# A shared SBUF port in the clocks of a program planner, and tiles split when they exist

## The chip, the cores and the metric

The kernel runs on one NeuronCore of a Trainium2 chip. Its engines each work through a queue of their own: TensorE (PE, with its weight loads shown apart as PEld), VectorE (DVE), ScalarE (ACT), GpSimd (POOL) and SyncE (SP), which here issues the DMA transfers. The metric is the device time of one execution in microseconds, less is better.

## What is computed

Two blocks of a network, one after the other, on 1,024 tokens of width 1,024, all in fp32. The first is a gated DeltaNet layer (8 query/key heads, 16 value heads of 128), the second holds 4 differential attention heads and 4 mLSTM heads whose outputs are merged. Cut to what matters for the time:

```python
def gated_deltanet(h, w_in, conv_w, a_log, dt_bias, norm_w, w_out):
    proj = h @ w_in
    qkv, z, b_lin, a_lin = jnp.split(proj, [...], axis=-1)
    qkv = jax.nn.silu(causal_depthwise_conv(qkv, conv_w))
    ...
    t_mat = lax.linalg.triangular_solve(l_mat, eye, left_side=True, lower=True, unit_diagonal=True)
    u = t_mat @ (v * beta);  w = t_mat @ (kb * jnp.exp(gc))
    ...
    def step(state, inp):                       # scan over chunks
        v_new = uc - wc @ state
        o = qd @ state + qkc @ v_new
        state = state * gl + kd.T @ v_new
    o = rms_norm(o, norm_w) * jax.nn.silu(z)
    return o @ w_out

x = x + gate * gated_deltanet(rms_norm(x) * (1 + scale) + shift, ...)    # shift, scale, gate from c @ ada_w
x = rms_norm(x, final_g)
proj = rms_norm(x, norm_pre) @ w_in_2           # 2nd block
ya = rms_norm(diff_attention(qa, ka, va)) * silu(za)
yb = rms_norm(sigmoid(ob) * mlstm(conv(qb), conv(kb), vb, ig, fg)) * silu(zb)
out = (sigmoid(ga) * (ya @ w_a) + sigmoid(gb) * (yb @ w_b)) @ w_out_2
return x + rms_norm(out, norm_post)
```

## The kernel before

**Products.** A large product (a projection of 128 columns, the output product) is cut into steps of three matmuls of 128x512: both operands are split into a high and a low half of fewer bits, and high times high, low times high and high times low are added in PSUM (`proj`, `yps`). A weight slab arrives by DMA (`wraw`); ACT rounds it to the high half (`whi`), and `split_lo` gives the subtraction for the low half (`wlo`) to POOL or to DVE, whichever the clocks below call free. The activations are split the same way (`hid_hi`, `hid_lo`; `ohl`; `h2hl`, whose source is `hv`).

**The first block** goes through eight head pairs, 0 to 7. Each pair has a chain: the convolution of q, k and v on DVE, six taps (`scalar_tensor_tensor` on `qT`, `kT`, `vT`, out of the PSUM tile of the projection), transposes on PE (`g`), decay tiles `E` from `gb`, matrices `U`, then the triangular solve (`levels`: `pG`, `pVT`, `pV`, small matmuls in bursts, and between them the rows `vtmp`, `Vl` on DVE, copied as `Ul` and passed through DRAM to `VTinv`), then the scan over chunks (`pst`, `po`, `pks`, `ptx`), and `finish` (norm, times z). The chain of the next pair's solve runs beside the scan of the one before. After pair 7 the output product is finished (`yps`).

**The second block** normalises the token halves r = 0 and 1 (`norm_tokens`: `x1`, `h2`, eight tiles `hv` each), projects them, and runs the gates of the mLSTM (`fgt`, `sp_z`, `sp_q`), the mLSTM chunks and the attention. From about 1,300 us on its products fill PE to the end.

**What sets the order.** Every instruction is recorded through `Engine.run`, so one line, L183, stands for all of them in the profile, and instructions are told apart by their tiles. The order on each engine is that of recording. `Pace` keeps an estimated clock for each engine while the program is recorded: `issue` starts an instruction at the later of its engine's clock and the time its operands are ready, and moves the clock on by `cost`. When the chain wants an instruction whose start is later than TensorE's clock, `Engine.run` calls `net.fill()`, which puts one step of background work (a product from the queue) ahead of it, and again, until TensorE's estimated clock has caught up or there is nothing to put. A product can be unable to go on: only two PSUM tiles hold products, and some of them wait in the plan for a pair's scan. Other work (weight splits, PSUM evacuations, the rows of the solve) waits in four lists and is recorded by `defer()` when the estimated clocks say that it would start without delay. A step's whole count of instructions is the same however these are mixed; the clocks decide the order, and which engine does a subtraction.

## Time and profile before

| | us |
|---|---|
| median of the runs (3) | 2027.89 |
| least and most of them | 2026.89, 2030.8 |
| the profiled execution | 2023.4 |
| its span | 2021.7 |
| PE busy in the span | 1942.5 |
| DVE, ACT, POOL busy | 1108.1, 909.0, 522.7 |

The profiled execution took 1.7 us more than its span, and 4.5 us less than the median. Two things besides work make up PE's time: the stretches in which it has nothing to run, and those in which it runs at a lower granted clock, in which it counts as busy.

### The profile page before, as it was taken

The numbers are of one execution on the slowest core, as the hardware profiler recorded it, in microseconds if no ns is written. First come the engines' busy times: TensorE is split into PE (matmuls) and PEld (weight loads), VectorE is DVE, ScalarE is ACT, GpSimd is POOL, SyncE is SP. The second block draws the span as 40 slices with busy tenths as digits, with TensorE's granted clock in tenths as the row PEclk, the third lists the DMA queues.
The fourth block names the chain that finished last, engine by engine and source line by source line (L and its number), as shares of the span: only waits on it lengthen the run. The fifth ranks groups of instructions, "written<-read, shape, count | busy, mean of one in ns | idle before, by whom it ended". The sixth has DMA issues, their size and how long they took to land. (4 is left out here: it accounts for less than half of the span.)

```text
span 2021.7 us, 29926 instructions
## 1 busy us (share of the span) xinstructions
PE 1942.5 (96%) x11105; PEld 1595.0 (79%) x11105; DVE 1108.1 (55%) x2639; ACT 909.0 (45%) x2103; POOL 522.7 (26%) x439
## 2 busy tenths in 40 slices
PE   6999999999999999999999799999999999999998
PEld 3778877877778787877778578888888888888887
DVE  3585877877858585843474665666434434000224
ACT  5444464544444544554355355565444444111222
POOL 2211111111111111123555221111334335323320
PEclk8999999999999999989999899999999999999999
DMA  8123313233313231324453311111111111211133
GB/s 281 46 53 67 80 46 82 59 72 89 78 43 72 48 72 35 69 106 144 170 207 106 93 43 32 32 27 32 48 53 48 53 37 47 52 47 48 51 116 125
DMA packets 262977, 152.13 MB, mean 75 GB/s; under 512 B 106314, under 2 KB 238123, under 8 KB 262831
## 3 DMA queue, kind: packets, MB, share of 16 engines
q1 hardware_dynamic: 262830, 150.22, 26.6%
q8 instruction: 88, 1.44, 0.3%
q14 instruction: 59, 0.48, 0.1%
HBM read 125.98 MB, written 24.20 MB: 74 GB/s over the span
## 5 line engine op out<-in xcount | busy, mean ns | idle before, releaser
L183 POOL TENSOR_TENSOR wlo<-wraw,whi 128x512 fp32r<-128x512 f32 x245 | 327.7, 1338 | 1259.1 <-ACT whi L183 1210.3
L183 PE MATMUL proj<-h2hl,whi 128*128 128x512 f32 (+1 forms) x1696 | 537.2, 400 | 7.5 <-ACT first L183 5.2
L183 ACT CAST whi<-wraw 128x512 fp32r<-128x512 f32 x292 | 178.6, 614 | 419.4 <-PE proj L183 212.7
L183 PEld LDWEIGHTS proj<-h2hl,whi 128*128 128x128 f32 (+1 forms) x1696 | 307.3, 189 | 66.7 <-ACT first L183 6.0
L183 PE MATMUL proj<-hid_hi,whi 128*128 128x512 f32 x768 | 336.6, 438 | 4.4 <-DVE vT L183 3.2
L183 PE MATMUL proj<-h2hl,wlo 128*128 128x512 f32 x832 | 326.2, 392 | 0.6 <-POOL wlo L183 0.6
L183 PE MATMUL proj<-hid_hi,wlo 128*128 128x512 f32 x768 | 304.4, 396 | 1.9 <-DVE wlo L183 1.9
L183 PE MATMUL proj<-hid_lo,whi 128*128 128x512 f32 x768 | 303.0, 395 | 0.0
L183 PEld LDWEIGHTS proj<-h2hl,wlo 128*128 128x128 f32 x832 | 156.6, 188 | 35.1 <-POOL wlo L183 1.1
L183 PE MATMUL yps<-whi,ohl 128*128 128x512 f32 x512 | 175.1, 411 | 6.7 <-ACT ohl L183 3.1
L183 PEld LDWEIGHTS proj<-hid_hi,wlo 128*128 128x128 f32 x768 | 145.8, 190 | 35.3 <-DVE wlo L183 2.5
L183 PEld LDWEIGHTS proj<-hid_hi,whi 128*128 128x128 f32 x768 | 146.4, 191 | 30.0 <-issue 5.4
L183 PEld LDWEIGHTS proj<-hid_lo,whi 128*128 128x128 f32 x768 | 147.1, 192 | 21.2
L183 PEld LDWEIGHTS yps<-whi,ohl 128*128 128x128 f32 x512 | 98.8, 194 | 30.4 <-DVE yT L183 3.3
L183 PE MATMUL yps<-wlo,ohl 128*128 128x512 f32 x256 | 102.8, 402 | 3.3 <-POOL wlo L183 2.5
L183 ACT ACT_TABLE_LOAD x75 | 96.2, 1283 | 20.1 <-DVE vT L183 8.7
L183 DVE TENSOR_TENSOR wlo<-wraw,whi 128x512 fp32r<-128x512 f32 x45 | 48.5, 1082 | 86.8 <-ACT whi L183 86.5
L183 ACT ACTIVATE qs<-pks,egc 128x128 f32<-128x128 f32 x112 | 35.0, 363 | 133.4 <-DVE xv L183 101.6
L183 DVE TENSOR_TENSOR vtmp<-Vl,Ul 128x126 f32<-128x126 f32 (+22 forms) x248 | 77.8, 314 | 9.5 <-DMA Ul<-ud 4.7
L183 DVE TENSOR_TENSOR merged<-proj,gate 128x1024 f32<-128x1024 f32 x8 | 9.8, 1220 | 130.0 <-PE proj L183 130.0
L183 ACT ACTIVATE prob<-prob,mx 128x128 f32<-128x128 f32 (+7 forms) x64 | 49.6, 776 | 59.1 <-DVE mx L183 57.6
L183 DVE TENSOR_TENSOR Vl<-Vl,vtmp 128x126 f32<-128x126 f32 (+22 forms) x248 | 71.1, 287 | 9.1
(372 smaller groups left out, 3382.0 us busy)
## 6 DMA issues: line engine op xcount, KB each, us to landing
wraw<-in_w_in SPq DMA_DIRECT2D x112, 256.0 KB, 2.8
wraw<-in_gdn_w_in SPq DMA_DIRECT2D x96, 256.0 KB, 2.8
wraw<-in_gdn_w_out SPq DMA_DIRECT2D x64, 256.0 KB, 3.2
adaw<-in_ada_w SPq DMA_DIRECT2D x16, 512.0 KB, 8.6
odram<-z SPq DMA_DIRECT2D x16, 512.0 KB, 3.0
oraw<-odram SPq DMA_DIRECT2D x30, 256.0 KB, 3.0
xin<-in_x SPq DMA_DIRECT2D x8, 512.0 KB, 4.6
Ul<-ud SPq DMA_DIRECT2D x16, 256.0 KB, 3.4
```

Source lines behind the costliest of these rows:

```text
L183: return f(*args, **kw)
```

## The change

`Pace` gets a record of the last twelve intervals in which VectorE and GpSimd, each, held the port to SBUF that they share (`port`). An instruction of GpSimd counts as using it unless it is a memset, one of VectorE if more than one of its inputs lies in SBUF and is larger than 128 elements in all (`shared`). Such an instruction's estimated start is moved behind every interval of the other engine that it falls into (`port_free`). The estimated cost of the scan operation is doubled. In the output product's last round, `split_h2` no longer splits the tile of h with a fixed number for each head, but the first tile that exists and is not yet split, and what is left is split after the round or where the tile is made. No instruction's arithmetic changes, and no instruction is added or taken away: on PE, 9,305 rows before and after.

```diff
--- before.py
+++ after.py
@@ -43,6 +43,7 @@
         self.dma = 0.0
         self.slots, self.seen, self.count = {}, {}, {}
         self.table = self.group = None
+        self.port = dict(vector=deque(maxlen=12), gpsimd=deque(maxlen=12))
 
     def box(self, ap):
 
@@ -96,6 +97,19 @@
             else:
                 tile_.append([p0, p1, f0, f1, 0.0, t, eng])
 
+    def shared(self, eng, op, ins):
+
+        if eng == "gpsimd":
+            return op != "memset"
+        return eng == "vector" and sum("PSUM" not in str(a.space) and a.ap[0][1] * a.ap[-1][1] > 128 for a in ins) > 1
+
+    def port_free(self, eng, start):
+
+        for a, b in sorted(self.port["gpsimd" if eng == "vector" else "vector"]):
+            if a <= start < b:
+                start = b
+        return start
+
     def cost(self, eng, op, outs, ins, args):
         n = 1
         for _, c in outs[0].ap[1:]:
@@ -113,6 +127,8 @@
                 return 0.03
             return max(0.42 * k, 0.84e-3 * m) if ins[0].dtype == F32R else max(1.68 * k, 1.68e-3 * m)
         if eng == "vector":
+            if op == "tensor_tensor_scan":
+                k *= 2
             return 0.07 + 1.04 * k + (0.06 if op == "scalar_tensor_tensor" else 0)
         if eng == "scalar":
             f = args.get("func", None)
@@ -150,7 +166,12 @@
             end = self.dma + 1.0
         else:
             f = dict(func=args[2]) if op == "activation" else {}
+            shared = self.shared(eng, op, ins)
+            if shared:
+                start = self.port_free(eng, start)
             end = self.t[eng] = start + self.cost(eng, op, outs, ins, f)
+            if shared:
+                self.port[eng].append((start, end))
         src = "dma" if op == "dma_start" else eng
         self.note(src, bo, end, True)
         self.note(src, bi, end, False)
@@ -1432,8 +1453,9 @@
             self.osplit(1, h + 2)
 
         def split_h2(h):
-            if 1 <= h <= KD:
-                self.h2split(h - 1, 0)
+            if h:
+                for k in self.unsplit_h()[:1]:
+                    self.h2split(k, 0)
 
         def gen_a():
             while not all(j.ready for j in self.held):
@@ -1456,9 +1478,15 @@
             yield from rounds(1, 0, every, split1)
             psum(1, 1)
             yield from rounds(1, 1, every, split_h2)
+            self.past.add("out")
+            for k in self.unsplit_h():
+                self.h2split(k, 0)
 
         self.out_a, self.out_b, self.out_c = Job(), Job(), Job()
         self.out_a.gen, self.out_b.gen, self.out_c.gen = gen_a(), gen_b(), gen_c()
+
+    def unsplit_h(self):
+        return [k for k in range(KD) if (k, 0) in self.hv and self.h2[k][0] is None]
 
     def h2split(self, k, r):
         v = self.hv[k, r]
@@ -1542,8 +1570,8 @@
             v = sp.tile([128, 512], F32, name="hv", tag="hv", bufs=8)
             nc.vector.tensor_scalar(v, p, self.p("norm_pre", k), None, op0=OP.mult)
             self.hv[k, r] = v
-            if r:
-                self.h2split(k, 1)
+            if r or "out" in self.past:
+                self.h2split(k, r)
             yield 1
```

What moves is told by the order of the two programs at three places. In all rows the line is `Engine.run`, L183 before and L204 now.

The first place is VectorE around 105 us, before the first pair's solve: the six taps of the convolution of v (`vT`), the matrices `U`, and the decay tiles `E` of the next pair. Before:

```order
L183 TENSOR_TENSOR b2d<-b_940,dl 128x8
L183 SCALAR_TENSOR_TENSOR U<-kk,b_940,E 128x128 x16
L183 SCALAR_TENSOR_TENSOR vT<-proj,convw,vT 128x511
L183 SCALAR_TENSOR_TENSOR E<-gb,gc,past_778 128x128 x4
L183 SCALAR_TENSOR_TENSOR vT<-proj,convw,vT 128x512
L183 SCALAR_TENSOR_TENSOR E<-gb,gc,past_778 128x128 x4
L183 SCALAR_TENSOR_TENSOR vT<-proj,convw,vT 128x510
L183 SCALAR_TENSOR_TENSOR vT<-proj,convw,vT 128x512
L183 SCALAR_TENSOR_TENSOR vT<-proj,convw,vT 128x509
L183 SCALAR_TENSOR_TENSOR vT<-proj,convw,vT 128x512
```

and now:

```order
L204 SCALAR_TENSOR_TENSOR vT<-proj,convw,vT 128x512
L204 COPY ktok<-g 128x512
L204 SCALAR_TENSOR_TENSOR vT<-proj,convw,vT 128x510
L204 TENSOR_SCALAR rk_956<-ssk 128x8
L204 RECIPROCAL rk_956<-rk_956 128x8
L204 TENSOR_TENSOR b_954<-beta,rk_956 128x8
L204 TENSOR_TENSOR b2d<-b_954,dl 128x8
L204 TENSOR_TENSOR b_954<-beta,rk_956 128x8
L204 TENSOR_TENSOR b2d<-b_954,dl 128x8
L204 SCALAR_TENSOR_TENSOR U<-kk,b_954,E 128x128 x16
L204 SCALAR_TENSOR_TENSOR vT<-proj,convw,vT 128x512
L204 SCALAR_TENSOR_TENSOR E<-gb,gc,past_781 128x128 x4
```

Three taps of six (two of them in these rows, the first stands just ahead) have moved ahead of the small operations on `rk` and `b` and of the sixteen on `U`.

The second place is TensorE at the end of the first pair's scan, between the last projection matmuls that can run there and the next pair's solve (`pG`); `g` are transposes, `v` what the scan gave, `vT` the next pair's values. Before, from the transposes of `v` on:

```order
L183 MATMUL g<-ident,v 128x128 x8
L183 MATMUL proj<-hid_hi,whi 128x512
L183 MATMUL proj<-hid_lo,whi 128x512
L183 MATMUL proj<-hid_hi,wlo 128x512
L183 MATMUL proj<-hid_hi,whi 128x512
L183 MATMUL proj<-hid_lo,whi 128x512
L183 MATMUL proj<-hid_hi,wlo 128x512
L183 MATMUL g<-ident,vT 128x128 x8
```

and now, the whole of it from the last projection matmul to `pG`:

```order
L204 MATMUL proj<-hid_hi,wlo 128x512
L204 MATMUL g<-ident,v 128x128 x16
L204 MATMUL g<-ident,vT 128x128 x4
L204 MATMUL gb<-grow,gsel 128x512
L204 MATMUL g<-ident,vT 128x128 x4
L204 MATMUL gb<-grow,gsel 128x512 x2
L204 MATMUL g<-ident,vT 128x128 x4
L204 MATMUL gb<-grow,gsel 128x512
L204 MATMUL g<-ident,vT 128x128 x4
L204 MATMUL pG<-VTinv,U 32x32 x32
```

From the last `po` of the scan to `pG` the program before has 48 projection matmuls, between the transposes for the most part, and now 18, all of them ahead of the transposes; the others stand earlier, most of them in the first pair's stage (108 in one run ahead of the first `pG` instead of 87, and 3 inside it).

The third place is TensorE at the start of the solve of pair 3; pair 6 reads much the same (at pair 4 some steps stood there already, with the `gb`). Before:

```order
L183 MATMUL pG<-VTinv,U 32x32 x32
L183 MATMUL gb<-grow,gsel 128x512
L183 MATMUL pVT<-G,Vinv 32x32
L183 MATMUL proj<-hid_hi,whi 128x512
L183 MATMUL proj<-hid_lo,whi 128x512
L183 MATMUL proj<-hid_hi,wlo 128x512
L183 MATMUL pV<-Vinv,G 32x32 x2
```

and now:

```order
L204 MATMUL pG<-VTinv,U 32x32 x32
L204 MATMUL proj<-hid_hi,whi 128x512
L204 MATMUL proj<-hid_lo,whi 128x512
L204 MATMUL proj<-hid_hi,wlo 128x512
L204 MATMUL proj<-hid_hi,whi 128x512
L204 MATMUL proj<-hid_lo,whi 128x512
L204 MATMUL proj<-hid_hi,wlo 128x512
L204 MATMUL pVT<-G,Vinv 32x32
L204 MATMUL proj<-hid_hi,whi 128x512
```

Two background steps stand between `pG` and the first `pVT` in the place of one `gb`, whose four stand ahead of the solve now.

## Rows read from the trace of the kernel before

**Rows 1.** This is the page of the kernel before: the span, the busy time of the engines (share of the span, instructions), and the clock that TensorE was granted in 40 equal slices of 50.5 us, in tenths (9 is 90% or more).

```profile
span 2021.7 us, 29926 instructions
...
PE 1942.5 (96%) x11105; PEld 1595.0 (79%) x11105; DVE 1108.1 (55%) x2639; ACT 909.0 (45%) x2103; POOL 522.7 (26%) x439
...
PEclk8999999999999999989999899999999999999999
```

**Rows 2.** This is busy time by stretches of the span. Columns: stretch, its length, then PE, PEld, DVE, ACT and POOL busy with their instructions, then the mean granted TensorE clock, the share of the DMA engines and GB/s. All times are us.

```profile
0.00:130.00 130.00, 106.11 (x586) 78.81 (x587) 69.00 (x172) 63.59 (x110) 30.78 (x33) 0.96 0.46 141
...
254.00:850.00 596.00, 578.81 (x4045) 477.96 (x4038) 436.94 (x1153) 300.14 (x843) 91.59 (x84) 0.98 0.26 62
850.00:1110.00 260.00, 247.52 (x1314) 200.36 (x1313) 127.37 (x178) 122.21 (x297) 116.00 (x83) 0.96 0.44 148
1110.00:1200.00 90.00, 73.92 (x334) 55.92 (x333) 61.17 (x124) 41.17 (x85) 25.15 (x20) 0.92 0.27 74
...
1300.00:2021.70 721.70, 714.77 (x3475) 597.15 (x3473) 264.37 (x616) 267.91 (x500) 220.44 (x188) 1.00 0.19 56
```

**Rows 3.** This is the waits of PE over the whole span, by what it waited for: us in total, times, the longest.

```profile
PE pks L183 <- DVE state L183: 6.8, 13, 1.1
...
PE pV L183 <- issue: 3.0, 4, 1.4
...
PE g L183 <- DVE fgt L183: 2.5, 1, 2.5
...
PE pG L183 <- DMA VTinv<-vtd: 0.7, 1, 0.7
```

**Rows 4.** This is one of the page's costliest groups: the low halves of weight slabs, as far as they are made on DVE (busy us, mean ns of one, idle time before them and what ended it).

```profile
L183 DVE TENSOR_TENSOR wlo<-wraw,whi 128x512 fp32r<-128x512 f32 x45 | 48.5, 1082 | 86.8 <-ACT whi L183 86.5
```

**Rows 5.** This is the timeline at 1150 us (start us, duration us, engine, line, operation, output<-inputs, form, count): a POOL and a DVE instruction side by side.

```profile
1150.36 1.28 POOL L183 TENSOR_TENSOR wlo<-wraw,whi 128x512 fp32r<-128x512 f32 x1 [5.44 <-ACT whi L183]
...
1150.41 1.29 DVE L183 TENSOR_TENSOR sp_z<-sp_z,sp_e 128x32 f32<-128x32 f32 x1
```

**Rows 6.** This is the instructions on DVE that touch the tile Ul between 230 and 330 us: duration in ns least/median/longest of two, and the first and last start.

```profile
L183 DVE COPY Ul<-Vl x2: 611/1072/1534, 234.2 to 322.5; 128x512 f32<-128x512 f32 x2
```

**Rows 7.** This is the timeline around 51 us, the first tokens projected (in brackets: idle time of the engine just before, and what ended it).

```profile
50.72 0.68 DVE L183 TENSOR_TENSOR wlo<-wraw,whi 128x512 fp32r<-128x512 f32 x1
...
51.46 0.50 PE L183 MATMUL proj<-hid_hi,wlo 128*128 128x512 f32 x1 [1.90 <-DVE wlo L183]
```

**Rows 8.** This is the timeline from 105 to 118 us: DVE between the first chunk's keys and the convolution of v, and the matmul of PE that waits for it.

```profile
105.87 0.22 DVE L183 TENSOR_SCALAR rk<-ssk 128x8 f32<-128x8 f32 x1 [3.01 <-ACT junk L183]
...
106.94 4.22 DVE L183 SCALAR_TENSOR_TENSOR U<-kk,b,E 128x128 f32<-128x128 f32 x16
...
115.10 2.71 DVE L183 SCALAR_TENSOR_TENSOR vT<-proj,convw,vT 128x510 f32<-128x510 f32 x4
...
117.95 0.47 PE L183 MATMUL proj<-hid_hi,whi 128*128 128x512 f32 x1 [3.24 <-DVE vT L183]
```

**Rows 9.** This is the timeline from the end of the first head pair's scan (the last `v<-po`) to the next pair's solve (`pG`): DVE's rows, and two matmuls that follow each other on PE.

```profile
238.96 0.43 DVE L183 TENSOR_TENSOR v<-po,qs 128x256 f32<-128x256 f32 x1 [2.83 <-PE po L183]
...
239.22 0.39 PE L183 MATMUL proj<-hid_hi,wlo 128*128 128x512 f32 x1
...
239.45 0.40 PE L183 MATMUL proj<-hid_hi,whi 128*128 128x512 f32 x1
...
242.16 3.60 DVE L183 TENSOR_TENSOR v<-v,ro 128x512 f32<-128x512 f32 x4
...
248.32 1.40 DVE L183 SCALAR_TENSOR_TENSOR z<-g,par,z 128x512 f32<-128x512 f32 x2
...
252.17 0.68 DVE L183 TENSOR_TENSOR v<-g,knrm 128x512 f32<-128x512 f32 x1
...
253.62 0.57 PE L183 MATMUL pG<-VTinv,U 32*32 32x32 f32 x22
```

**Rows 10.** This is busy time and clock as in rows 2, for 16 us around the solve of pairs 1, 3, 4 and 6.

```profile
254.00:270.00 16.00, 15.80 (x255) 12.43 (x248) 10.86 (x26) 9.95 (x13) 3.26 (x5) 1.00 0.08 20
437.00:453.00 16.00, 14.95 (x237) 10.99 (x235) 8.68 (x20) 6.68 (x9) 1.28 (x1) 0.79 0.25 76
556.00:572.00 16.00, 14.48 (x190) 11.41 (x189) 5.72 (x13) 2.96 (x5) 1.38 (x1) 0.79 0.07 18
757.00:773.00 16.00, 12.80 (x222) 9.83 (x223) 7.53 (x20) 6.31 (x8) 1.29 (x1) 0.79 0.07 18
```

**Rows 11.** This is the timeline at 557 us, between `pG` and the first `pV` of pair 4's solve.

```profile
556.84 1.13 DVE L183 SCALAR_TENSOR_TENSOR E<-gb,gc,past 128x128 f32<-128x128 f32 x4 [0.88 <-PE gb L183]
...
558.07 0.22 PE L183 MATMUL pV<-Vinv,G 32*32 32x32 f32 x2 [1.27 <-issue]
```

**Rows 12.** This is the timeline at 871 us, inside the last pair's solve.

```profile
870.99 0.80 PE L183 MATMUL yps<-whi,ohl 128*128 128x512 f32 x1 [3.06 <-ACT ohl L183]
...
871.48 1.35 DVE L183 TENSOR_TENSOR ohl<-oraw,ohl 128x512 fp32r<-128x512 f32 x1 [2.53 <-ACT ohl L183]
```

**Rows 13.** This is the timeline at 1116 us, where the first token half of the second block is normalised and the accumulators of v are emptied (`first`).

```profile
1114.84 1.15 ACT L183 ACTIVATE h<-x,r 128x1024 f32<-128x1024 f32 x1 [1.49 <-DVE x L183]
...
1116.20 0.60 ACT L183 ACTIVATE first<-proj 128x512 f32<-128x512 f32 x1
...
1116.85 1.22 PE L183 MATMUL proj<-h2hl,whi 128*128 128x512 f32 x2 [4.05 <-ACT first L183]
```

## The prediction

> **What bounds the kernel now.** The page comes first [rows 1]: TensorE (PE) is busy for 1942.5 of 2021.7 us, and no other engine for more than 55%. So work is not what the change can save, since it neither adds nor removes a matmul; what it can move is the rest: the 79 us in which PE has nothing to run, and the time lost while its clock is granted at half. The busy times by stretch split the span [rows 2]. From 1300 us to the end PE is busy for 714.77 of 721.70 us at clock 1.00, so the last third has nothing to give. Before it, PE stands idle for 23.9 us up to 130, 17.2 from 254 to 850, 12.5 from 850 to 1110 and 16.1 from 1110 to 1200. I take a stretch's clock loss as its length times what its mean clock lacks of 1: 0.04 x 130 = 5, 0.02 x 596 = 12, 0.04 x 260 = 10, 0.08 x 90 = 7 us, an estimate that is right only where PE was busy. About 70 us of idle time and 34 us of clock can be moved at all. Part of it has nothing to do with the planner's clocks: the scan's waits for `state`, thirteen at 0.5 us [rows 3], are one dependency each.
>
> **Why the planner's clocks are wrong.** One pair of rows shows it [rows 5]: at 1150.41 DVE starts a 128x32 product of two SBUF tiles, which takes 1.29 us and ends just behind POOL's subtraction (1150.36 + 1.28). The same operation on 128x512 takes 0.68 us when it runs alone [rows 7] and 1.08 on the mean of 45 [rows 4]. A planner that doesn't know it believes DVE free a microsecond early, records too little background work ahead of what DVE must deliver, and PE waits. The change makes that delay visible, so more steps of three matmuls stand ahead of such waits. The amount of background is fixed, though: each step spent here is missing elsewhere.
>
> **What the Trainium skill adds.** The page "SBUF — State Buffer", section "Who interferes with whom", says that the pair of ports is an exclusive lock, that an operation of DVE with two SBUF inputs meets GpSimd's reads, and that copies and scalar operations with one input can meet them too in their fast modes. The trace agrees with the last: the same copy `Ul<-Vl` took 611 and 1534 ns [rows 6]. The change's `shared` leaves copies out. By it the sum below stands; by the page the copy of each of seven solves would still be planned up to 0.92 us early, which would take at most 6.5 us off the gain; PE's only wait for what hangs on that copy, `VTinv`, is 0.7 us [rows 3], so I take nothing.
>
> **The change part by part.** The edits of the clock, of the scan's cost and of the order in which tiles of h are split cost nothing by themselves; they act through the order. I went along PE's waits and read in the new order what stands there.
>
> 1. *The wait of 1.90 us at 51.46* [rows 7]. DVE makes the low half of the weights only at 50.72. Now this subtraction stands earlier on its engine, and a product of z fills PE meanwhile. −1.9 (bounds −1.9 and 0).
>
> 2. *The wait of 3.24 us at 117.95* [rows 8]. Before, DVE is idle for 3.01 us ahead of 105.87, then does 16 `U` (4.22 us), and the last four taps begin only at 115.10. Now three of six taps stand ahead of `U`, in that idle time, each some 0.68 us: the last tap ends 2 to 3 us earlier. −3.0 (−3.2 and −1).
>
> 3. *The end of the first scan* [rows 9]. This is where the spent steps are missing. Before, 48 projection matmuls at 0.23 us each (239.22 to 239.45) and some 30 transposes fill the 14.7 us from `v<-po` at 238.96 to `pG` at 253.62 and PE never waits. Now only 18 are left, all ahead of the transposes, since the next product needs a PSUM tile that the taps of `kT` have yet to empty. So PE follows DVE's chain: from the start of `v<-po` the norm needs 3.2 us to 242.16, four `v<-v,ro` at 0.68 to 0.90 (the one as in [rows 7], the other the 3.60 for four with POOL beside them) 2.8, then six taps at 0.68 (2.71 over 4 in [rows 8]) and four `z` at 0.70 make 6.9, then the `v` and `E` operations that release PSUM for the last transposes and for `pG`, two at 0.68 and ten at 0.26 (4.22 over 16 in [rows 8]), 4.0: `pG` at about +17 us. PE has 18 x 0.23 + 32 x 0.12 + 4 x 0.25 = 9 us of work in that. It waits 8 us more than before, in pieces of about 1 us. The windows around four solves show what such waits bring: around the solves of pairs 3, 4 and 6, where PE was idle for 1.1, 1.5 and 3.2 of 16 us, the mean clock is 0.79 [rows 10] (so 6.7 us at the lower of its two levels, 1.2 in place of 2.4 GHz), and around that of pair 1, with 0.2 us idle, it is 1.00. I take one such stretch behind the hole, 3.4 us. +11.4 (bounds +5: the idle time alone, and shorter; +17: 12 us idle and a lower clock for 10).
>
> 4. *The solves of pairs 3, 4 and 6* [rows 10]. Before, a `gb` stands between `pG` and `pV` there. Its four `E` on DVE must empty its PSUM tile before `pV` can write one: at pair 4 the last ends at 556.84 + 1.13 = 557.97 and `pV` starts at 558.07, after 1.27 us put down to "issue" [rows 11]; the four waits of that name make 3.0 us [rows 3]. At pairs 3 and 6 there is besides nothing to run while `pG` is emptied. Now the `gb` stand ahead of `pG`, and two steps (6 x 0.23 = 1.4 us) and one more (0.7 us) fill the two places, as steps did at pair 1, where PE waits 0.2 us in all. The idle time over that of pair 1 is 0.9 + 1.3 + 3.0 = 5.2 us, and the clock costs 3 x 0.21 x 16 = 10 us. All of it would be −15. The solve's bursts of small matmuls remain, and other waits can bring the clock down; I take four fifths, −12 (bounds −15 and −5: the idle time alone).
>
> 5. *The last pair's solve* [rows 12]. There is no projection left. Before, PE waits 3.06 us for the high half `ohl`; now 20 transposes stand in a row without a matmul between them, each four waiting for a 0.68 us evacuation on DVE, which also gets more of the `ohl` subtractions (22 instead of 17; 1.35 us at 871.48, beside POOL's), and 48 `yps` follow. About 5.4 us idle instead of 3.1: +2.3 (0 and +7, with a longer stretch of lower clock).
>
> 6. *1000 to 1050 us, the first token half's transposes.* 45 `yps` stand between them instead of 39, and the tiles `hv` come later, for which the new rule of splitting is needed. The waits there change places: 0 (−3 and +3).
>
> 7. *The accumulators of v* [rows 13]. PE waits 4.05 us until `first` (1116.20 + 0.60) is done, which stands on ACT behind an `h` of 1.15 us and a short cast. Now `first` stands ahead of both. −1.5 (−2 and 0).
>
> 8. *The gates* [rows 3]. Ahead of the transposes of `fgt` stand 36 matmuls instead of 27, because the planner sees the two blocked operations like that at 1150 us [rows 5]: 9 x 0.23 = 2.0 of the 2.5 us, and a lower clock of 3.4 us behind it that costs 1.7. The scan operation, whose doubled cost belongs here, ends nothing that PE waits for in the rows I read: nothing. −3.7 (−4.2 and −1).
>
> **The sum.** −1.9 − 3.0 + 11.4 − 12 + 2.3 + 0 − 1.5 − 3.7 = −8.4 us. Against the profiled execution's 2023.4 that is 2015.0; the median of the runs is 4.5 us above that execution, so about **2020 us**.
>
> **The rivals.** A measurement here tells from no change what is above 0.2%, 4 us.
>
> *The holes decide (slower).* Terms 3 and 5 are one mechanism: background is spent earlier, and at the end of scan 0 and at the last solve PE runs on DVE's pace. The other terms give −22. The two holes cost 13.7 in my sum; from 22 on the change is a loss, and from 26 a measurable one. With 12 us idle and the lower clock for 10 us at the first (17), and 7 at the second, they cost 24; the same lower clock, brought on by any wait of the chain, then also stays at the solves, which give back their idle time alone (−5): together +9, 2037 us; with my term 4 it is +2. For it speaks that the whole chain there is DVE's and that POOL's weight splits block it; against it that the steps not run there must be run somewhere, and the places with waits are where the planner now puts them. Chance 0.22.
>
> *All the waits of the solves go (faster by more).* Term 4 at −15, term 3 at +5, term 5 at 0: −20, 2008 us. For it speaks pair 1, which has neither wait nor low clock with the same filling; against it the 3.2 us at pair 6. Chance 0.18.
>
> *The waits only change places (same).* Wherever PE is filled now, it had a reason to wait that comes back a few steps later, since the dependencies on DVE are as long as ever: term 4 at −5, term 8 at −1, the others as above: +1, so about 2029. For it: PE is at 96%, and the same steps are merely dealt out otherwise. Chance 0.20.
>
> **How the numbers follow.** The forecast, 2014 to 2024 us, has 0.40. The range from 2007 to 2034 takes in the second rival and the last, stops 3 us short of the first one's full price, and leaves about 2 in 10 out. Faster by over 4 us: the forecast but for its upper end and the second rival, 0.56; within it 0.21; slower 0.23.
>
> **What the profile of the changed kernel would show.** Right: no wait of `proj` for `vT` near 118 or for `wlo` near 51; a stretch of some 12 us after the first scan with PE about half busy and a lower clock behind it; mean clock 1.00 around the solves of pairs 3, 4 and 6, with PE at 15.8 of 16; the wait for `fgt` under 1 us. Wrong: PE busy throughout the end of the first scan; clocks of 0.79 at the solves although the filling stands there; new waits of PE, for `whi`, `wlo` or a transpose's evacuation, in the chunks that now look filled; a change after 1300 us.

## The result and the profile after

The changed kernel takes 2015.56 us in the median of 6 runs, against 2030.61 for the kernel before on the same chips: a ratio of 0.9929 (95% interval 0.9914 to 0.9943), so 0.7% or some 14 us faster. The profiled execution took 2012.22 us with a span of 2010.5, 11.2 less than before.

The page of the changed kernel, with the lines that answer to [rows 1]:

```profile
span 2010.5 us, 29928 instructions
...
PE 1938.9 (96%) x11105; PEld 1589.9 (79%) x11105; DVE 1125.5 (56%) x2646; ACT 905.3 (45%) x2100; POOL 515.6 (26%) x435
...
PEclk9999989999999999999999899999999999999999
```

PE does the same work; its busy time of 1938.9 us is 3.6 less than before, with a mean granted clock of 0.989 in place of 0.983 over the span. POOL has four instructions fewer and DVE seven more. The 8 in the sixth slice (251 to 302 us) is the hole behind the first scan that the prediction spoke of; the 8 at 860 us [rows 1] is a 9 now, that at 1110 us stays.

The busy times by stretches, as in [rows 2] and [rows 10] (busy PE, PEld, DVE, ACT, POOL, then granted clock, DMA share, GB/s): the end of the first scan, the solves of pairs 1, 3, 4 and 6, and the stretch from the end of the seventh scan to the last solve.

```profile
244.00:264.00 20.00, 14.95 (x60) 9.71 (x59) 17.31 (x38) 7.27 (x12) 1.28 (x1) 0.70 0.59 135
264.00:280.00 16.00, 16.00 (x254) 12.41 (x255) 9.18 (x15) 5.47 (x9) 1.69 (x2) 0.85 0.13 35
454.00:470.00 16.00, 15.92 (x267) 12.45 (x266) 7.07 (x14) 4.66 (x7) 1.52 (x2) 1.00 0.71 188
561.00:577.00 16.00, 15.65 (x184) 12.70 (x174) 10.53 (x25) 4.49 (x7) 2.07 (x2) 1.00 0.24 68
765.00:781.00 16.00, 16.00 (x263) 12.36 (x262) 4.80 (x7) 4.80 (x8) 1.26 (x1) 1.00 0.46 132
845.00:879.00 34.00, 27.34 (x122) 20.83 (x122) 18.35 (x29) 12.82 (x24) 9.72 (x8) 0.90 0.42 100
```

The solves of pairs 3, 4 and 6 have lost most of their idle time (0.43 us are left in all, 5.77 before) and their lower clock (0.79 before). Around that of pair 1 PE is never idle, but its clock is 0.85. At the two ends of scans PE is idle for 5.05 of 20 and 6.66 of 34 us, at clocks of 0.70 and 0.90.

PE's waits over the span, as in [rows 3]:

```profile
PE g L204 <- DVE z L204: 8.8, 7, 3.6
...
PE proj L204 <- ACT first L204: 3.6, 2, 2.4
...
PE pst L204 <- ACT wd L204: 2.9, 4, 0.7
PE proj L204 <- DVE vT L204: 2.8, 1, 2.8
...
PE g L204 <- DVE fgt L204: 0.7, 1, 0.7
...
PE pks L204 <- DVE state L204: 0.3, 1, 0.3
```

The waits named "issue" are gone, and of those for `state`, 6.8 us before, 0.3 are left. New are those for `z`, 8.1 of their 8.8 us at the two ends of scans.

**Lost time.** The spans of two stages can't be subtracted where background moves between them. PE runs the same 11,105 matmuls in all these kernels, so I took from each trace the time from the start of a matmul to the start of the next, less the median of that for its form (its shape) in the trace of before (0.23 us for a 128x512 matmul). The medians sum to 1862.3 us for every kernel, and what is left, 149.4 us before and 138.0 after, is what was lost: waits, lower clock and short stalls together. A solve is counted from its first `pG` to the first `pst` of the scan behind it. By stage, in us, with the kernels of the experiments (the run's number ahead of its label):

```
stage                          before  after    e1    e2    e5    e7   e10   e11   e12
start to the first solve         30.5   28.5  33.8  32.4  27.3  33.8  29.1  31.1  28.2
first solve and scan              3.7    3.5   3.9   3.5  25.5  15.5   4.4   4.4   3.5
end of scan 0 to solve 1          0.5   11.3   1.4   1.3  11.1  12.9   1.3   0.5  11.3
solves of pairs 1 to 6           35.6   20.5  18.0  38.1  24.1  37.9  19.1  23.1  22.0
scans of pairs 1 to 6            15.0    8.8  15.1   7.3   7.4   5.7  13.7  11.3   9.7
ends of scans 1 to 5              4.6    9.2   7.7   6.6   7.0  12.3   9.9   5.5   6.9
end of scan 6, solve 7           10.3   13.9   9.0  10.0   9.2   9.8   6.6   6.6  11.9
last scan to the token halves    14.5   12.0  15.9  14.1   9.5  20.1  12.4  12.7  11.0
token half, gates                26.3   20.9  26.7  22.6  21.5  28.0  21.9  21.2  22.1
the rest                          8.3    9.3   8.5  13.7  10.9   8.3  10.8  11.0  11.0
sum                             149.4  138.0 139.9 149.6 153.5 184.4 129.4 127.4 137.7
```

Each column is one execution, and some of it is that execution's own: before, e1, e4, e7 and e9 have the same order on PE, DVE, ACT and POOL up to the first solve, and lost 30.5, 33.8, 33.9, 33.8 and 33.6 us up to there. The last section shows where that comes from.

### The profile page after: what moved, and what is told of

Read it like the earlier page. It is cut to its first block, busy times and chain, and to the rows that moved or that the text cites. A ratio compares the mean times of both kernels' runs of the same rounds, so it can differ in the third digit from the quotient of the medians.

```text
span 2010.5 us, 29928 instructions
## 1 busy us (share of the span) xinstructions
PE 1938.9 (96%) x11105; PEld 1589.9 (79%) x11105; DVE 1125.5 (56%) x2646; ACT 905.3 (45%) x2100; POOL 515.6 (26%) x435
## 5 line engine op out<-in xcount | busy, mean ns | idle before, releaser
L204 POOL TENSOR_TENSOR wlo<-wraw,whi 128x512 fp32r<-128x512 f32 x245 | 324.5, 1325 | 1261.5 <-ACT whi L204 1186.4
L204 PE MATMUL proj<-h2hl,whi 128*128 128x512 f32 (+1 forms) x1696 | 536.2, 399 | 8.4 <-ACT first L204 3.6
L204 PEld LDWEIGHTS proj<-h2hl,whi 128*128 128x128 f32 (+1 forms) x1696 | 306.6, 188 | 67.0 <-ACT first L204 4.4
L204 ACT CAST whi<-wraw 128x512 fp32r<-128x512 f32 x292 | 178.5, 613 | 391.4 <-PE proj L204 176.3
L204 PE MATMUL proj<-hid_hi,whi 128*128 128x512 f32 x768 | 335.0, 436 | 3.2 <-DVE vT L204 2.8
L204 PE MATMUL proj<-h2hl,wlo 128*128 128x512 f32 x832 | 325.8, 392 | 0.3 <-POOL wlo L204 0.3
L204 PE MATMUL proj<-hid_hi,wlo 128*128 128x512 f32 x768 | 303.1, 395 | 0.0
L204 PE MATMUL proj<-hid_lo,whi 128*128 128x512 f32 x768 | 301.7, 393 | 0.0
L204 PEld LDWEIGHTS proj<-h2hl,wlo 128*128 128x128 f32 x832 | 156.4, 188 | 34.7 <-POOL wlo L204 0.7
L204 PE MATMUL yps<-whi,ohl 128*128 128x512 f32 x512 | 172.5, 404 | 4.7 <-DVE yT L204 3.2
L204 PEld LDWEIGHTS proj<-hid_hi,wlo 128*128 128x128 f32 x768 | 145.0, 189 | 33.1 <-POOL wlo L204 0.3
L204 PEld LDWEIGHTS proj<-hid_hi,whi 128*128 128x128 f32 x768 | 145.9, 190 | 29.7 <-issue 4.8
L204 PEld LDWEIGHTS proj<-hid_lo,whi 128*128 128x128 f32 x768 | 146.2, 190 | 21.6
L204 PEld LDWEIGHTS yps<-whi,ohl 128*128 128x128 f32 x512 | 96.7, 190 | 28.1 <-DVE yT L204 3.3
L204 ACT ACT_TABLE_LOAD x75 | 96.2, 1283 | 25.7 <-DVE kT L204 23.7
L204 PE MATMUL yps<-wlo,ohl 128*128 128x512 f32 x256 | 101.3, 396 | 3.1 <-POOL wlo L204 2.4
L204 ACT ACTIVATE qs<-pks,egc 128x128 f32<-128x128 f32 x112 | 34.9, 363 | 133.9 <-DVE xv L204 97.9
L204 DVE TENSOR_TENSOR vtmp<-Vl,Ul 128x126 f32<-128x126 f32 (+22 forms) x248 | 86.7, 350 | 7.2 <-DMA Ul<-ud 2.1
L204 DVE TENSOR_TENSOR wlo<-wraw,whi 128x512 fp32r<-128x512 f32 x45 | 51.0, 1134 | 59.3 <-ACT whi L204 59.1
L204 DVE TENSOR_TENSOR merged<-proj,gate 128x1024 f32<-128x1024 f32 x8 | 9.8, 1221 | 131.2 <-PE proj L204 130.0
L204 ACT ACTIVATE prob<-prob,mx 128x128 f32<-128x128 f32 (+7 forms) x64 | 49.6, 776 | 64.4 <-DVE mx L204 61.2
L204 DVE TENSOR_TENSOR Vl<-Vl,vtmp 128x126 f32<-128x126 f32 (+22 forms) x248 | 70.3, 284 | 9.1
```

Source lines behind the costliest of these rows:

```text
L204: return f(*args, **kw)
```

## The experiments

My theory after the result: the change gains by what stands inside the solves, at the scans and behind 935 us, and it loses part of that again in two holes, since its clocks spend background earlier. The rivals: any longer estimate for VectorE does the same; the place of the `gb` alone does it; the holes are the price and can't be had back.

**e1: the kernel before, and the `gb` recorded ahead of every solve.**

```diff
         yield from self.drain(self.cold)
+        yield from self.drain(self.side)
 
         G = sp.tile([128, 16, 32], F32, name="G", tag="Vl", bufs=1)
```

> The kernel before with one line more: ahead of every solve the queued gb/E items are recorded, so that no gb stands between pG and pV; no port model, no other edit. Theory (the gain at the solves comes from the place of the gb and the steps that follow, not from the port itself): the lost time of the solves of pairs 1 to 6 falls from 34 to about 18 us as in the changed kernel, the clock of 0.79 around them goes, and no hole opens behind the first scan, since 75 matmuls stand there: 12 to 18 us faster than before, ratio 0.991 to 0.994. Rival (what counts is that the planner sees blocked operations): the waits come back elsewhere, ratio 0.998 to 1.002.

Ratio 0.9925 (0.9912 to 0.9938): one line, and the time of the whole change. The windows of its trace at the end of the first scan and the solves of pairs 3, 4 and 6:

```profile
242.00:265.00 23.00, 22.47 (x115) 17.97 (x114) 17.58 (x35) 8.51 (x14) 3.99 (x3) 1.00 0.55 134
449.00:465.00 16.00, 16.00 (x268) 12.75 (x267) 10.31 (x24) 5.05 (x8) 2.08 (x2) 1.00 0.19 52
556.00:572.00 16.00, 15.65 (x145) 12.63 (x135) 12.51 (x28) 3.99 (x6) 1.29 (x1) 1.00 0.26 72
759.00:775.00 16.00, 16.00 (x264) 12.30 (x263) 5.05 (x11) 5.05 (x8) 2.45 (x2) 1.00 0.13 33
```

No hole (22.47 of 23 us busy), and the solves as full as in the changed kernel. The solves of pairs 1 to 6 lose 18.0 in place of 35.6 us, while scans and everything behind 850 us lose what they lost before. So the port model isn't needed for the largest gain; it came to a like order there by another way. Nor is it a matter of single traces: the mean clocks of e1's six executions are 0.986 to 0.991, those of the kernel before beside them 0.981 to 0.987.

**e2: the kernel before with a uniformly longer estimate for VectorE.**

```diff
-            return 0.07 + 1.04 * k + (0.06 if op == "scalar_tensor_tensor" else 0)
+            return 0.07 + 1.12 * k + (0.06 if op == "scalar_tensor_tensor" else 0)
```

> The kernel before with every operation of VectorE estimated 8% longer a column (1.12 in place of 1.04), which is the mean of what the port costs it, and no port model. Rival theory (any more pessimistic clock of VectorE gives the gain): ratio 0.992 to 0.995, the solves' lost time halved. Theory (it matters where the planner sees the delay): steps move at random places, gb stand inside the solves of pairs 3, 5 and 7 still with one step only, lost time of the solves within 6 us of before, ratio 0.997 to 1.003.

Ratio 0.9977 (0.9964 to 0.9990): a small gain, not the change's, for the one size of estimate that was tried. The lost time of the solves is 38.1 us, and at pairs 2, 4 and 6, where three matmuls and a `gb` stand between `pG` and `pV`, the windows look as those of before at pair 6:

```profile
357.00:373.00 16.00, 13.41 (x224) 10.14 (x224) 8.54 (x20) 6.29 (x8) 1.27 (x1) 0.79 0.15 39
555.00:571.00 16.00, 14.83 (x181) 11.58 (x182) 7.05 (x20) 3.85 (x6) 1.26 (x1) 0.64 0.13 35
759.00:775.00 16.00, 13.71 (x236) 10.80 (x235) 7.11 (x18) 6.20 (x8) 1.26 (x1) 0.79 0.09 22
```

With e1 and before this gives what a solve costs by what stands in its gap, from the last of the opening `pG` to the first `pV`. Nine matmuls and no `gb`: 2.7 to 3.4 us in twelve solves (pairs 1 to 7) of after, e1 and e2, and 4.9 in the one behind the first hole, where the lower clock goes on. Nine to twelve and one `gb`: 5.2, 2.9 and 3.7 before, 3.2 in after, 3.0 and 3.7 in e2. Twelve and two `gb`: 7.5. Three or none and one `gb`: 7.3 and 8.9 before, 11.0, 10.3 and 7.4 in e2. So one `gb` beside nine or more matmuls costs little, and the dear solves are those with three or no matmuls and one `gb`, and that with twelve and two. No run has few matmuls and no `gb`, so the share of each is not shown. Nor does the gap tell all: of the 5.2 us of pair 1 before, 2.5 lie behind the solve's last `pV`, and in e7 below all gaps hold nine matmuls and no `gb`, yet the solves of pairs 1 to 6 lose 4.8 to 7.3 us each, 2.1 to 4.8 of it behind that point.

**e3: the changed kernel without the doubled cost of the scan operation.**

```diff
-            if op == "tensor_tensor_scan":
-                k *= 2
```

> The changed kernel without the doubled estimate of the scan operation. The order differs only behind 1130 us. Theory (the doubling is worth little): the wait for the forget gates and the two behind it change by 0 to 2 us, ratio to the kernel before 0.992 to 0.994, the changed kernel's own. Rival (the doubling carries the 4 us gained at the gates): 3 to 4 us slower than the changed kernel, ratio 0.994 to 0.996.

Ratio 0.9925 (0.9909 to 0.9940), the changed kernel's own. The stages from the first token half to the gates lost 23.0 us in place of 20.9, which the ratio can neither confirm nor exclude. In the order that the program writes, the other half of the question is answered without a run: with the doubled cost and the new splitting of h but no port model, PE's, ACT's and POOL's instructions stand as in the kernel before, row for row, and DVE's but for two. So the time moved by the port model. The new splitting is what lets its order be written: the fixed number would ask for a tile of h that doesn't exist yet.

**e4: the port model from the output product on, and the `gb` as in e1.** `late` starts as False; the line on the `gb` is e1's.

```diff
     def shared(self, eng, op, ins):
 
+        if not self.late:
+            return False
...
     def out_phase(self):
...
+        self.pace.late = True
```

> The port model switched on only when the output product begins (before that the clocks are those of the kernel before), the gb recorded ahead of every solve as in the first run of this group, the other edits of the change kept. Theory (the port model's early part gains at the solves and pays for it with two holes, at the ends of the first and of the seventh scan): no hole behind the first scan, solves as in the changed kernel, the last third as in the changed kernel: lost time 126 to 132 us in place of 149 before and 138 now, ratio 0.988 to 0.991. Rival (the holes only move the filling, and what isn't lost there is lost in other places): ratio as the changed kernel's, 0.992 to 0.995.

Ratio 0.9920 (0.9906 to 0.9934), lost time 140.0: the same as e1. My expectation was missed by 8 us, and the ratio is the rival's. From the last scan to the token halves it lost 16.7 us and from there to the gates 23.7, in place of the changed kernel's 12.0 and 20.9. Behind 850 us the model gains little when it is switched on as late as there.

**e5: the changed kernel with the key product third in the queue.** Its two holes have no product to run, because the one under way has filled its PSUM tile and the other waits for a scan. So I took another order of the background products.

```diff
-QUEUE = "vvzqzk"
+QUEUE = "vvkzqz"
```

> The changed kernel with one edit: the next pair's key product but one stands third among the background products of a pair instead of last (vvkzqz for vvzqzk), so that at the end of a scan another product than one that waits for that scan is under way. 39 and 75 projection matmuls stand then, among the transposes, where the changed kernel's two holes are (18 and 9, ahead of them). Theory (the two holes, 10.8 and 10.7 us of lost time, are empty places of the queue and can be filled without a loss elsewhere): both fall under 2 us each, the rest stays, 16 to 21 us faster than the changed kernel, ratio to the kernel before 0.982 to 0.986. Rival (the amount of filling is fixed, so the holes move): other places lose as much, ratio 0.990 to 0.995.

Ratio 1.0031 (1.0017 to 1.0044): slower than before. The second hole closed (0.7 us lost there in place of 11.2, though the solve behind it lost 8.5 in place of 2.7), but at the first nothing was won, and the first scan ran nearly without filling: 9 projection matmuls stand in it instead of 132. Its window and that behind it:

```profile
171.00:236.00 65.00, 51.84 (x426) 38.41 (x424) 36.06 (x126) 30.83 (x100) 4.52 (x6) 0.92 0.14 30
236.00:261.00 25.00, 17.50 (x103) 14.14 (x102) 19.29 (x45) 7.50 (x16) 2.69 (x2) 0.80 0.63 145
```

and, in the timeline of the first, PE's longest wait, behind a row of the solve on DVE:

```profile
207.35 1.19 PE L204 MATMUL pks<-state,kT 128*128 128x256 f32 x2 [3.97 <-DVE vtmp L204]
```

The 39 projection matmuls that now stand behind the scan come too late for its hole, whose longest wait is ahead of the first transpose:

```profile
242.48 1.12 PE L204 MATMUL g<-ident,v 128*128 128x128 f32 x4 [6.09 <-DVE v L204]
```

The key product of pair 2 may not be emptied before scan 0 is done; put third, it stands in PSUM during that scan and holds up all that follows it. So the hole at the end of the scan stayed (11.1 us lost), and the first solve and scan lost 25.5 us where the changed kernel loses 3.5. Both expectations failed: the rival's reason, that filling won at one place is missing at another, was right, but its range was not; it lost far more than it won.

**e6: the changed kernel, with copies and scalar operations counted by the port model.**

```diff
+        if ins and op in ("tensor_copy", "tensor_scalar") and "PSUM" not in str(ins[0].space):
+            return eng == "vector" and ins[0].ap[0][1] * ins[0].ap[-1][1] > 128
```

> The changed kernel whose port model also counts copies and scalar operations with one input in SBUF larger than 128 elements. Theory (nothing that PE waits for hangs on such a copy): orders differ at some 20 places, ratio to the kernel before as the changed kernel's, 0.991 to 0.995. Rival (the omission costs up to 0.92 us at each of seven solves): 0.988 to 0.991.

Ratio 0.9917 (0.9904 to 0.9931), lost time 138.1 against 138.0. The difference to the changed kernel is inside the interval; a gain of 6 us is not excluded by the ratio, but the trace has none.

**e7 and e8: two more places for the key product.** e7 is e1 with the queue of e5, without the port model; e8 is e5 with `vkvzqz`.

> The kernel before with the gb recorded ahead of every solve and with the order of the background products of the fifth run (vvkzqz), and no port model. Theory: with the gb out of the way the solves lose 3 us each as in the changed kernel, and at the end of the scans 36 to 75 matmuls stand among the transposes; what the port model adds in the first 850 us is then small, so it comes within 4 us of the fifth run if that loses its holes. Rival (the port model's clocks gain by themselves at the scans and the start): 5 to 10 us slower than the fifth run.

> As the fifth run, with the key product second (vkvzqz): 39 and 48 matmuls in the places of the two holes, none longer than 8 transposes without one between. Theory of the holes: within 4 us of the fifth run, ratio 0.982 to 0.987. Rival (the order of the products acts by chance, through other waits): more than 5 us apart.

Ratios 1.0152 (1.0137 to 1.0167) and 1.0268 (1.0248 to 1.0288). e7 missed both its theory and its rival by far; e8 is 50 us from e5, as its rival allowed; that chance is the reason, as the rival had it, is not shown. The first scan holds 36 and 0 projection matmuls. In the windows over it PE is idle for 7.6 and 23.9 us, against 13.2 with the 9 matmuls of e5:

```profile
171.00:232.00 61.00, 53.44 (x449) 41.20 (x449) 38.50 (x131) 31.96 (x100) 5.85 (x7) 1.00 0.17 37
```

```profile
172.00:247.00 75.00, 51.15 (x376) 37.86 (x375) 39.17 (x131) 29.94 (x98) 1.93 (x4) 0.68 0.15 29
```

That is not all of it: e7's solves of pairs 1 to 6 lose 20 us more than e1's, and of the 58 us that e8 loses beyond e5 only 22 lie ahead of the solve of pair 1. Ahead of a stretch whose length a chain sets, what may run in it counts, not how even the queue looks.

**e9 and e10: the port model switched off where the first hole is made.** e9 has it on from the end of the first scan, e10 also up to the convolution of the first pair's v; both have the `gb` of e1 and the test of `late` in `shared` that e4 shows. The edit is that of e10; e9 starts with `late` False and has no other line that sets it so.

```diff
+        self.late = True
...
         yield from self.prep_v(0, V[0])
+        self.pace.late = False
...
             self.past.add(("scan", j))
+            self.pace.late = True
```

> The changed kernel whose port model is switched on only when the first scan is over, with the gb recorded ahead of every solve: up to the end of the first scan the order is that of the first run (e1_gb_first), behind it the clocks know the port. 75 matmuls stand among the transposes behind the first scan and 39 behind the seventh, no gb stands inside a solve. Theory (the first hole is made by background spent in the first pair's stage, and costs nothing elsewhere if it isn't spent there; the port's gain at the scans, 6 us, and behind 935 us, 8 us, needs the model on there): lost time 122 to 130 us, ratio 0.984 to 0.989. Rival (as in the fifth run, whatever is filled at one place is missing at another): ratio 0.990 to 0.995.

> As e9_from_scan0, but the port model is also on up to the convolution of the first pair's v, so that only the first solve and the first scan are planned without it. Theory: as e9_from_scan0, and 2 us better at the start, where the wait of 1.9 us at 51 us goes: ratio 0.983 to 0.988. Rival (the first pair's stage already spends too much with the model on): a hole of 10 us behind the first scan, or a scan without filling, ratio above 0.990.

Ratios 0.9882 (0.9863 to 0.9901) and 0.9884 (0.9869 to 0.9899), both faster than the changed kernel; lost time 133.7 and 129.4, above what I had expected of e9, and e10's ratio just above its range. The first hole is gone (1.3 us) and doesn't come back elsewhere; at the end of scan 6 they lose 3.9 in place of 11.2. What I had put down as the model's gain at the scans didn't come: 14.2 and 13.7 us, as before.

**e11: e10 without its edit on the `gb`.**

> As e10_off_first_pair without its edit on the gb: only the port model, switched off for the first solve and the first scan. 48 matmuls stand behind the first scan, the solves of pairs 1 and 5 have one gb inside but 9 and 15 matmuls. Theory (what pays is that the first scan's end keeps its background; where the clocks know the port the solves fill themselves): within 4 us of e10_off_first_pair, ratio 0.986 to 0.990. Rival (the place of the gb is needed too): 5 us or more slower than it, ratio above 0.991.

Ratio 0.9864 (0.9844 to 0.9883), 2000.09 us: the fastest of all, and within the noise of e10. Its page, and the windows at the end of the first scan and the solve behind it:

```profile
span 1999.8 us, 29930 instructions
...
PE 1929.5 (96%) x11105; PEld 1588.0 (79%) x11105; DVE 1117.6 (56%) x2644; ACT 907.2 (45%) x2100; POOL 519.1 (26%) x437
...
PEclk8999999999999999999999999999999999999999
```

```profile
240.00:255.00 15.00, 15.00 (x83) 12.16 (x82) 12.36 (x21) 4.64 (x10) 2.68 (x2) 1.00 0.81 179
255.00:271.00 16.00, 15.79 (x265) 12.45 (x264) 10.85 (x26) 9.55 (x12) 3.27 (x5) 1.00 0.15 45
```

Its solves lose 4 us more than e10's (a `gb` in two of them), its scans and their ends 7 less. So where the clocks know the port, the edit on the `gb` gives nothing more.

**e12: the changed kernel, with the `gb` as in e1.**

> The changed kernel with the gb recorded ahead of every solve, and the port model on throughout. 18 matmuls, none among the transposes, stand behind the first scan as in the changed kernel, and 39 behind the seventh. Theory (the first hole is set in the first pair's stage and stays): lost time behind the first scan 10 to 12 us again, behind the seventh 3 to 5 in place of 11, ratio 0.988 to 0.991. Rival (the hole closes or moves with any other order): under 4 us behind the first scan.

Ratio 0.9917 (0.9901 to 0.9933), just above my range. The first hole is there again, as my theory had it, to the tenth of a microsecond (11.3 us of lost time):

```profile
243.80:263.70 19.90, 14.89 (x57) 9.63 (x56) 17.25 (x37) 7.24 (x12) 1.29 (x1) 0.70 0.59 136
```

Behind the seventh scan it lost 4.8 us, but 7.1 in the last solve in place of 2.7. Of the kernels that know the port in the solves and scans, only those with the model off in the first pair's stage (e9, e10, e11) have no first hole.

## Why the prediction was right, and where it was not

The forecast was −8.4 us by the traces, about 2020 us; they show −11.2, and the comparison of all runs −14, at 2015.56 us. So the gain was larger than the sum, and several steps missed in opposite ways. By its steps, against the table:

1 and 2. *The start*, forecast −4.9: 30.5 became 28.5. The wait at 51 us is gone. That for `vT` is not, and this step failed. The rows of the changed kernel's timeline where [rows 8] stood:

```profile
111.96 0.40 PE L204 MATMUL proj<-hid_hi,wlo 128*128 128x512 f32 x1
...
113.67 1.40 DVE L204 SCALAR_TENSOR_TENSOR vT<-proj,convw,vT 128x509 f32<-128x509 f32 x2
...
115.21 0.67 PE L204 MATMUL proj<-hid_hi,whi 128*128 128x512 f32 x1 [2.85 <-DVE vT L204]
```

The last tap ends at 115.07, 2.7 us earlier than before, as the step said. But PE came to the point earlier too, at 112.36 instead of 114.71, since the wait at 51 us had gone and its filling stood at other places. I moved one side of the wait only. The −2.0 is, besides, against an execution of the kernel before that did well here: the four others of the same order lost 33.6 to 33.9, and against these the start gains 5 us. With 33.8 for 30.5 the difference of the traces would be 14.5 us, an estimate near the 14 of all runs.

3. *The end of the first scan*, forecast +11.4: 0.5 became 11.3. PE's waits in it:

```profile
249.55 0.66 PE L204 MATMUL g<-ident,v 128*128 128x128 f32 x4 [0.55 <-DVE v L204]
252.12 1.11 PE L204 MATMUL g<-ident,v 128*128 128x128 f32 x4 [1.92 <-DVE z L204]
254.10 1.11 PE L204 MATMUL g<-ident,v 128*128 128x128 f32 x4 [0.86 <-DVE z L204]
...
260.91 1.09 PE L204 MATMUL g<-ident,vT 128*128 128x128 f32 x4 [0.78 <-DVE E L204]
```

The idle time is 5 us and not 8, in pieces of up to 1.9, and the lower clock lasts some 17 us and not 6.7 (by the windows, 0.30 x 20 and 0.15 x 16 us are lacking to full clock, 8.4 in all, at half; 2.4 of it falls into the solve of pair 1). PE was idle for less because four transposes took 1.1 us at the lower clock and not 0.66 as in the first row, in what would have been waits. And DVE's chain is longer than I had it:

```profile
244.38 0.43 DVE L204 TENSOR_TENSOR v<-po,qs 128x256 f32<-128x256 f32 x1 [2.08 <-PE po L204]
...
256.58 0.68 DVE L204 TENSOR_TENSOR v<-g,knrm 128x512 f32<-128x512 f32 x1
...
259.63 2.16 DVE L204 SCALAR_TENSOR_TENSOR E<-gb,gc,past 128x128 f32<-128x128 f32 x8 [0.35 <-PE gb L204]
...
263.97 0.76 PE L204 MATMUL pG<-VTinv,U 32*32 32x32 f32 x21
```

From `v<-po` to `pG` it took 19.6 us where I had 17. Up to the first `v<-g` it came as forecast (12.2, forecast 12.9); behind it stand three `v` and sixteen `E` where I had counted two and ten, and DVE waits 0.9 us for PE, so that the tail is 7.4 and not 4.0. That the stage came out within 0.6 us was luck: less idle time and more lower clock than I had cancel.

4. *The solves of pairs 3, 4 and 6*, forecast −12 of at most −15: 23.7 became 9.5 us, −14.2. The clock stayed up in all three, as in e1. The reason, a `gb` in the gap and too little beside it, is borne out as a whole by e1, whose one line takes the `gb` out of the gap and lets nine matmuls fill it. How it divides is not shown. Beside the `gb` stood three matmuls at pair 3, none at pair 6 and twelve at pair 4. One `gb` beside nine or twelve matmuls goes with 0 to 2 us more (before, e2), but at pair 4 a second `gb` stood just ahead of `pV`, and 7.5 us were lost in spite of the twelve.

5. *The last pair*, forecast +2.3: 10.3 became 13.9, +3.6. The hole is larger than I thought, 11.2 us, but the solve behind it lost 2.7 in place of 9.8. These are the windows over it, before and after:

```profile
863.90:889.70 25.80, 22.60 (x289) 17.92 (x289) 8.59 (x12) 13.59 (x35) 4.22 (x3) 0.80 0.17 59
```

```profile
878.90:899.10 20.20, 20.20 (x296) 16.28 (x296) 6.22 (x9) 9.96 (x31) 3.81 (x3) 1.00 0.49 163
```

The wait of 3.06 us for `ohl` is gone from it, with 42 `yps` in place of 30 and six projection matmuls, and so is the lower clock. The 42 `yps` alone don't do it: e12 has them too and no wait in that solve, but a clock of 0.78, and lost 7.1.

6. *The first token half's transposes*, forecast 0: 13.8 became 11.4 between the last scan and the first transpose of the second block.

7 and 8. *`first` and the gates*, forecast −1.5 and −3.7: 16.0 became 14.6, and 10.3 became 6.4 for the two stages around `fgt`; both within 0.3 us. The wait for `first` is 2.4 us in place of 4.1, that for `fgt` 0.7 in place of 2.5. That the scan's doubled cost gives nothing was right as far as the ratio tells (e3); the wait for `fgt` is 0.7 us there too.

*Not in the sum:* the scans of pairs 1 to 6 lost 6.2 us less and their ends 4.6 more. I had called the waits for `state` one dependency each; they went from 6.8 to 0.3 us, as more matmuls stand ahead of `pks` (4.4 between `pst` and `pks` on the mean, 3.7 before). They are not the whole of it: in e10 they are 1.9 us. The port's knowledge alone isn't the cause: e9 and e10 have the model on there and lose 14 us. e5 and e7 lose 7.4 and 5.7 with other queues, so it hangs on which products run beside the scans; how, stays open.

*The rivals.* "The holes decide" had its mechanism right and its weight too large: steps 3 and 5 cost 14.4 us together by the table (10.8 and 3.6), where 22 were needed. "All the waits go" was at hand: e11, without the first hole, is 28 us faster than before. "The waits only change places" failed, since it gave the three solves 5 us and they gained 14.2. Of the signs named, the clock and the busy time at the three solves and the wait for `fgt` came; the wait for `vT` stayed, and the stretch behind the first scan was 20 us at three quarters busy and not 12 at half. That the gain needs the knowledge of the port is shown only in part: e1 got the same time without it, e11 the double with it, and a longer estimate of another size than e2's was not tried.

## What to carry to other kernels

A planner that fills a busy engine's waits deals out a fixed budget: see at each stage what is left to run there, and what may not run yet, before trusting a gain at another. A change of a planner's clocks is worth comparing with the one-line edit of the order that its largest gain comes from. And lost time per instruction, by stage, adds up over kernels whose stages don't line up, where idle time and clock told apart do not.

## What was not expected of the hardware

The lower clock isn't a fixed answer to a wait. Up to the first solve the rows of PE, DVE, ACT and POOL stand in the same order before and in e1, and the waits at 51 and 118 us are the same 1.9 and 3.2 us in both traces. The windows over them, in e1 and then in the kernel before:

```profile
50.00:57.00 7.00, 5.31 (x42) 2.65 (x43) 1.29 (x2) 1.98 (x4) 1.27 (x1) 0.76 0.16 40
118.00:126.00 8.00, 5.32 (x20) 4.22 (x21) 5.74 (x14) 3.86 (x4) 1.29 (x1) 0.79 0.36 90
```

```profile
50.00:57.00 7.00, 5.54 (x54) 3.76 (x55) 1.89 (x5) 2.95 (x6) 1.28 (x1) 1.00 0.16 40
118.00:126.00 8.00, 7.12 (x35) 5.77 (x36) 6.34 (x19) 3.78 (x5) 1.27 (x1) 1.00 0.15 38
```

In e1's execution the clock is 0.76 and 0.79 there, in that of before 1.00. Those of e4, e7 and e9, with the same order and the same two waits, have e1's 0.76 and 0.79. These two stretches of lower clock, 3.4 us each, are the 3 us by which the start of before lost less than theirs. So the clock's part of a single trace's difference is not all the kernel's, and a forecast can give it by its size but not by its place. Why the execution of before kept its clock is not known.
